# One decoder block on one core: the SBUF pad is left out and the arena of working tiles has 69 tiles, not 68

## The chip, the core and the metric

The kernel runs on one core of a Trainium2 chip. The metric is the time on the device in microseconds (us). The kernel before took 1007.3 us in the median of three runs (1007.09 to 1009.21).

A core has five engines that work beside each other: PE (TensorE, matmuls; its loads of the stationary operand are listed as PEld), DVE (VectorE), ACT (ScalarE), POOL (GpSimd) and SP (SyncE, which issues DMAs here). Each runs its own instructions in a fixed order and waits for others by semaphores. SBUF is the memory that the engines work on; PSUM is the memory that PE writes.

## The reference

One layer of a decoder trunk on 512 tokens of width 1024, batch 1, in float32:

```
h = rmsnorm(x)
h @ w_in  ->  gated linear attention (q, k, v, output gate, forget gate)
              dilated attention, 3 groups of 4 heads (window, dilation) (128,1) (512,4) (2048,16)
              two merge gates
A = gated linear attention in chunks of 64 tokens, 4 heads, dk 128, dv 256
B = the three groups, combined by their softmax denominators
x += (sigmoid(gA) * (A @ w_o_gla) + sigmoid(gB) * (B @ w_o_attn)) @ w_out
x += relu(rmsnorm(x) @ w_mlp1)^2 @ w_mlp2
x += sigmoid(rmsnorm(x) @ w_pg) * (p @ w_pp)
out = rmsnorm(x)
```

For a chunk, with decays a, the gated linear attention carries a state S = diag(a) S + k^T v from chunk to chunk and gives o = q S (the kernel works it out for pairs of chunks).

## The kernel before

Every large product is made of matmuls on numbers that are split into a high part (`hi`, rounded) and a low part (`lo`, the rest): three matmuls hi·hi, hi·lo, lo·hi per tile (`three`, L239 issues them). Weights come in 209 pieces of 128 x 1024 by DMA into the six buffers `w`; for each piece ACT makes `hi` (L225) and DVE makes `lo` (L220). Many of the projections use a scheme of seven products instead of eight (`strassen`), with sums of weight pieces made by DVE (L205, L211) and by DMAs that add to what is in `w` (L197, L208).

The order of each engine's instructions is that of the program. PE runs the large products in pieces of 8 matmuls (`run`), and after each piece `step()` lets the side work go one step: generators in the list `side` (two at a time) and small functions in `later`. So the small matmuls and the DVE and ACT work of the attention parts are interleaved with the large products. Waits on an engine hold up all that stands behind.

The side work of this case is `gla(h)`, one generator for each of the four heads of the gated linear attention. Heads 2 and 3 run together, beside the large products of the merge gate `gb` (410 to 460 us of the profiled run). In a head's program: transposes of the keys (L855), the chunk products (L861, L863), the sums of k^T v of pairs (L876 and L887, recorded at L815), the states after one, two and three pairs `s[1]`, `s[2]`, `s[3]` (L884, L885, L889; DVE), their high parts `ss[p][:, 0:256]` (L891; ACT) and low parts `ss[p][:, 256:512]` (L894; DVE), and the outputs (`outs`, matmuls recorded at L815), which read `ss`. L344 is the low part of an operand of these products (`split_lo`), L329 the addition of a finished product to a sum (`add`), L1006 the sigmoid of a gate.

Memory: pools of SBUF follow each other. `const` and `st` hold small tiles; then the pad (L146); then `wst` (the six `w`), `wsp` (5 `hi`, 4 `lo`, 4096 bytes in each partition), and `ar`, the arena: `NU` tiles of 128 x 512 numbers, 2048 bytes in each partition, named `u` or, for split operands, `ur`. All other working tiles are taken from the arena when the program asks for one and given back after their last use. Who gets a tile that another has had waits until the readers and writers of the former one have passed. In the built program before, the first `w` begins at byte 26624 of the partition, `hi` at 51200, `lo` at 71680 and the arena at 88064, all multiples of 2048; of the small tiles, `rstd` begins at 21248 and 23296, `ones_r` at 19616, `ident` at 17408 and `whs` at 18080. The most arena tiles in use at one time, in program order, are 68 of 68; that is in the stretch of `gla(2)` and `gla(3)`.

Of the kernel before, what the change touches and what calls it, by code (L numbers as in the profile page):

```python
# [10 lines left out]
F32 = mybir.dt.float32  # L11
# [8 lines left out]
P = 128  # L20
# [106 lines left out]
C_LN2, C_LN3, C_BA, C_GN, C_LN1, C_LO, C_N = 0, 8, 16, 20, 28, 36, 38  # L127
W0, W12 = 384, 256

NU, NW, PIECE, WAYS = 68, 5, 8, 2  # L130

NPAD = 208

NRAW = 6

# [4 lines left out]
def block_kernel(ctx, tc, xT, ws, pT, wts, wha, wa2, vec, lnf, rel, onehot, ident_d, mask_d, out):  # L140
# [2 lines left out]

    const = ctx.enter_context(tc.tile_pool(name="const", bufs=1))
    st = ctx.enter_context(tc.tile_pool(name="st", bufs=2))
    const.tile([P, NPAD], F32, name="pad")  # L146
    wst = ctx.enter_context(tc.tile_pool(name="wst", bufs=NRAW))
    wsp = ctx.enter_context(tc.tile_pool(name="wsp", bufs=1))
    ar = ctx.enter_context(tc.tile_pool(name="ar", bufs=NU))
# [1218 lines left out]
```

## Time and profile before

| | before |
|---|---|
| median of three runs | 1007.3 us (1007.09 to 1009.21) |
| the profiled run, its own time | 1008.85 us |
| its span, first to last instruction | 1006.7 us |
| PE busy | 984.2 us (98%) |
| DVE busy | 673.6 us (67%) |
| ACT busy | 525.9 us (52%) |
| mean granted clock of PE | 0.991 |

The page gives the busy time of each engine and then the same in 40 equal slices of some 25.2 us, a digit for tenths, and a row PEclk with the granted clock of PE in tenths (1.0 is 2.4 GHz, 0.5 is 1.2 GHz). A view of windows gives these numbers for any stretch; the timeline gives single instructions, with the idle time of the engine before them and what ended it in brackets. A busy PE isn't a PE at its peak: matmuls overlap, and their ends are modelled.

### The profile page before, as it was taken

Reading aid. Unit: us, or ns where it says so; the run is one execution under the profiler, and the core shown is the slowest. Engines: PE = TensorE matmul, PEld = TensorE weight load, DVE = VectorE, ACT = ScalarE, POOL = GpSimd, SP = SyncE. Lnnn points to the kernel's source line nnn. Section 1 sums busy time; section 2 is a strip of 40 time slices with the busy share of each in tenths; the row PEclk is TensorE's granted clock in tenths of the full one; section 3 lists DMA queues with packets and bytes.
Section 4 is the critical chain, followed back from the end, with each engine's and each line's share of the span. In section 5 each row is a group of like instructions: output and inputs, shape, how many; then the busy total and the mean of one; then the engine's idle time right before and its main releaser. Section 6 shows DMA issues by size and latency. Waiting matters only on the chain.

```text
span 1006.7 us, 15530 instructions
## 1 busy us (share of the span) xinstructions
PE 984.2 (98%) x6228; PEld 898.8 (89%) x6228; DVE 673.6 (67%) x948; ACT 525.9 (52%) x875; POOL 80.4 (8%) x116
## 2 busy tenths in 40 slices
PE   9999999999999999889999999999999999999996
PEld 7788999999998999879988888999998888888885
DVE  7776675566677677858955689778877544743553
ACT  7335547645546665646632346655666434443633
POOL 0230000010000101012002001101000000000000
PEclk9999999999999999979999999999999999999999
DMA  8463461463366355426536425665654322433102
GB/s 303 129 212 83 106 173 40 103 147 106 86 167 167 115 133 146 112 63 177 163 121 193 121 63 148 156 179 131 163 147 147 89 100 81 151 103 102 46 1 84
DMA packets 38168, 127.31 MB, mean 126 GB/s; under 512 B 4883, under 2 KB 6495, under 8 KB 38096
## 3 DMA queue, kind: packets, MB, share of 16 engines
q1 hardware_dynamic: 27504, 92.51, 28.3%
q0 software_dynamic: 8864, 30.66, 15.6%
q10 hardware_dynamic: 1728, 3.15, 0.8%
q8 instruction: 49, 0.80, 0.3%
q14 instruction: 23, 0.19, 0.1%
HBM read 122.06 MB, written 6.07 MB: 127 GB/s over the span
## 4 chain that ended last, share of the span: by engine, by line
PE 91%; DVE 5%; issue 2%; ACT 1%; DMA 0%; POOL 0%; SPq 0%; POOLq 0%; DVEq 0%; ACTq 0%
PE mmt L239 73%; PE smt L239 9%; PE smt L815 2%; DVE lo L220 1%; PE smt L759 1%; PE smt L686 1%; PE smt L861 1%; PE mmt L453 1%; DVE w L205 0%; PE mmt L454 0%; DMA u<-in_xT_dram 0%; PE mmt L452 0%; PE smt L863 0%; PE smt L776 0%; PE smt L775 0%
## 5 line engine op out<-in xcount | busy, mean ns | idle before, releaser
L239 PE MATMUL mmt<-ur,hi 128*128 128x256 f32 (+1 forms) x2784 | 610.3, 315 | 0.0
L239 PEld LDWEIGHTS mmt<-ur,hi 128*128 128x128 f32 x2784 | 461.4, 192 | 31.8 <-issue 1.9
L239 PE MATMUL mmt<-ur,lo 128*128 128x256 f32 (+1 forms) x1392 | 438.0, 315 | 0.5 <-DVE lo L220 0.5
L220 DVE TENSOR_TENSOR lo<-w,hi 128x1024 fp32r<-128x1024 f32 x230 | 278.9, 1221 | 121.8 <-PE mmt L239 71.9
L225 ACT ACTIVATE hi<-w 128x1024 fp32r<-128x1024 f32 x230 | 240.7, 1053 | 133.1 <-issue 65.1
L239 PEld LDWEIGHTS mmt<-ur,lo 128*128 128x128 f32 x1392 | 266.6, 191 | 16.4 <-DVE lo L220 0.9
L239 PE MATMUL mmt<-hi,ur 128*128 128x256 f32 (+1 forms) x640 | 156.1, 334 | 0.0
L336 ACT ACTIVATE ur<-u 128x512 fp32r<-128x512 f32 x136 | 80.2, 621 | 91.6 <-DVE u L1036 30.9
L239 PEld LDWEIGHTS mmt<-hi,ur 128*128 128x128 f32 x640 | 119.8, 215 | 5.6
L344 DVE TENSOR_TENSOR ur<-u,ur 128x512 fp32r<-128x512 f32 x135 | 89.0, 688 | 26.9 <-ACT ur L336 22.7
L239 PE MATMUL mmt<-lo,ur 128*128 128x256 f32 (+1 forms) x320 | 106.1, 332 | 0.6 <-DVE lo L220 0.6
L239 PE MATMUL smt<-ur,hi 128*128 128x512 f32 x272 | 83.7, 389 | 0.0
L311 ACT ACTIVATE u<-mmt 128x512 f32<-128x512 f32 x84 | 49.9, 594 | 53.5 <-PE mmt L239 52.9
L329 DVE TENSOR_TENSOR u<-u,mmt 128x512 f32<-128x512 f32 (+1 forms) x84 | 52.5, 652 | 29.2 <-PE mmt L239 29.1
L239 PEld LDWEIGHTS mmt<-lo,ur 128*128 128x128 f32 x320 | 68.8, 215 | 3.6 <-DVE lo L220 1.0
L239 PEld LDWEIGHTS smt<-ur,hi 128*128 128x128 f32 x272 | 51.1, 188 | 10.6
L239 PE MATMUL smt<-ur,lo 128*128 128x512 f32 x136 | 53.0, 390 | 0.0
L208 POOL DMA_DIRECT2D w<-in_wts_dram x21 | 18.2, 868 | 311.0 <-DVE w L205 234.4
L1146 ACT ACTIVATE u<-u 128x256 f32<-128x256 f32 x64 | 23.0, 409 | 36.5 <-DVE u L1137 36.5
L197 POOL DMA_DIRECT2D w<-in_wts_dram x21 | 18.6, 888 | 204.8 <-DMA w<-in_wts_dram 76.9
L239 PEld LDWEIGHTS smt<-ur,lo 128*128 128x128 f32 x136 | 25.5, 188 | 5.3
L205 DVE TENSOR_TENSOR w<-w 128x1024 f32<-128x1024 f32 x21 | 25.7, 1225 | 0.7
(204 smaller groups left out, 723.4 us busy)
## 6 DMA issues: line engine op xcount, KB each, us to landing
w<-in_wts_dram SPq DMA_DIRECT2D x167, 512.0 KB, 3.8
w<-in_wts_dram POOLq DMA_DIRECT2D x42, 512.0 KB, 5.7
u<-in_xT_dram SPq DMA_DIRECT2D x8, 256.0 KB, 4.6
y_dram<-u ACTq DMA_DIRECT2D x8, 256.0 KB, 2.6
u<-y_dram POOLq DMA_DIRECT2D x8, 256.0 KB, 5.6
u<-in_xT_dram POOLq DMA_DIRECT2D x8, 256.0 KB, 7.4
cb_dram<-c_dram POOLq DMA_DIRECT2D x4, 448.0 KB, 6.2
u<-in_ws_dram SPq DMA_DIRECT2D x8, 192.5 KB, 4.6
```

The lines of the kernel that those rows point to most:

```text
L197: GP.dma_start(w, wts[UNIT[f"{q}.A22"]], accum_op=OP.add)
L205: V.tensor_tensor(w, w, raw[f"{q}.A11"], op=OP.add)
L208: GP.dma_start(w, wts[UNIT[f"{q}.A21"]], accum_op=OP.add)
L220: V.tensor_tensor(lo, w, hi.bitcast(F32), op=OP.subtract)
L225: S.activation(hi, w, AF.Copy)
L239: TE.matmul(o, lhsT=l, rhs=r, start=a, stop=b, skip_group_check=shared)
L311: S.activation(sums[c], bank[b], AF.Copy, scale=-scale if c[0] else scale)
L329: V.tensor_tensor(out, s, ps, op=OP.subtract if m else OP.add)
L336: S.activation(hi, x, AF.Copy)
L344: V.tensor_tensor(lo, x, hi.bitcast(F32), op=OP.subtract)
L815: TE.matmul(o, lhsT=l[a][:, lc], rhs=r[b], start=start and i == 0, stop=stop and i == 2)
L1146: S.activation(hid[j][:, halves(t)], s[:, halves(n)], AF.Square)
```

## The change

The pad of 208 numbers (832 bytes in each partition) is left out, and `NU` is 69. The names of lines above are those of the kernel before; in the kernel after, lines from L134 on stand three lines earlier. In the built program after, the small tiles of `const` and `st` and the large pools begin 832 bytes lower: `w` at 25792, `hi` at 50368, `lo` at 70848, the arena at 87232. Each of these large pools begins 1216 bytes above a multiple of 2048. In the stretch of `gla(2)` and `gla(3)` up to 69 arena tiles are in use.

```diff
@@ -127,9 +127,7 @@
 C_LN2, C_LN3, C_BA, C_GN, C_LN1, C_LO, C_N = 0, 8, 16, 20, 28, 36, 38
 W0, W12 = 384, 256
 
-NU, NW, PIECE, WAYS = 68, 5, 8, 2
-
-NPAD = 208
+NU, NW, PIECE, WAYS = 69, 5, 8, 2
 
 NRAW = 6
 
@@ -143,7 +141,6 @@
 
     const = ctx.enter_context(tc.tile_pool(name="const", bufs=1))
     st = ctx.enter_context(tc.tile_pool(name="st", bufs=2))
-    const.tile([P, NPAD], F32, name="pad")
     wst = ctx.enter_context(tc.tile_pool(name="wst", bufs=NRAW))
     wsp = ctx.enter_context(tc.tile_pool(name="wsp", bufs=1))
     ar = ctx.enter_context(tc.tile_pool(name="ar", bufs=NU))
```

The instructions of every engine are the same and stand in the same order. What differs is which former tile a new one of the arena takes the place of, and so the waits. This is DVE's program in the states of heads 2 and 3, before (the names are out<-in with their numbers; s[2] of head 3 is u_4542, its s[1] u_4541, and ur_4522 is the first `ss` of head 2; in brackets the semaphores waited for, PE_49 being PE's):

```order
L344 TENSOR_TENSOR ur_4518<-u_4340,ur_4484 128x512 [waits DVE_49,PE_49,Activation_49]
L884 COPY u_4520<-smt_4477 128x256 [waits PE_49]
L885 SCALAR_TENSOR_TENSOR u_4521<-u_4520,dab_4259,smt_4477 128x256 [waits DVE_49,Activation_49]
L344 TENSOR_TENSOR ur_4539<-u_4353,ur_4506 128x512
L884 COPY u_4541<-smt_4499 128x256 [waits DVE_49]
L885 SCALAR_TENSOR_TENSOR u_4542<-u_4541,dab_4283,smt_4499 128x256 [waits DVE_49,PE_49]
L220 TENSOR_TENSOR lo_4552<-w_4101,hi_4488 128x1024 [waits DMASW7_49]
L205 TENSOR_TENSOR w_4101<-w_4101,w_4324 128x1024 [waits DVE_49]
L329 TENSOR_TENSOR u_4447<-u_4447,mmt_4271 128x512
L889 SCALAR_TENSOR_TENSOR u_4520<-u_4521,dab_4259,smt_4527 128x256
L889 SCALAR_TENSOR_TENSOR u_4541<-u_4542,dab_4283,smt_4548 128x256
L894 TENSOR_TENSOR ur_4522<-u_4520,ur_4522 128x256 [waits Activation_49]
```

And the same place after (every number of a tile is one lower):

```order
L341 TENSOR_TENSOR ur_4517<-u_4339,ur_4483 128x512 [waits DVE_49,PE_49,Activation_49]
L881 COPY u_4519<-smt_4476 128x256 [waits DVE_49,PE_49]
L882 SCALAR_TENSOR_TENSOR u_4520<-u_4519,dab_4258,smt_4476 128x256 [waits DVE_49,PE_49]
L341 TENSOR_TENSOR ur_4538<-u_4352,ur_4505 128x512 [waits Activation_49]
L881 COPY u_4540<-smt_4498 128x256
L882 SCALAR_TENSOR_TENSOR u_4541<-u_4540,dab_4282,smt_4498 128x256 [waits DVE_49]
L217 TENSOR_TENSOR lo_4551<-w_4100,hi_4487 128x1024 [waits DMASW7_49]
L202 TENSOR_TENSOR w_4100<-w_4100,w_4323 128x1024 [waits DVE_49]
L326 TENSOR_TENSOR u_4446<-u_4446,mmt_4270 128x512
L886 SCALAR_TENSOR_TENSOR u_4519<-u_4520,dab_4258,smt_4526 128x256
L886 SCALAR_TENSOR_TENSOR u_4540<-u_4541,dab_4282,smt_4547 128x256
L891 TENSOR_TENSOR ur_4521<-u_4519,ur_4521 128x256 [waits Activation_49]
```

No row has moved. The second state of head 3 (L885, after: L882) waited for PE and no longer does: before, its tile is one that an operand of head 2's first output matmuls had (`smt_4634`); after, it is one that head 3's own `at` had, which PE doesn't read. The first row waits for PE in both, but by the values of the semaphores for different matmuls: before, for head 3's group of the third pair; after, for head 2's group ahead of it.

## Rows read from the trace of the kernel before

**Rows 1.** The page: PE's busy time, and its granted clock in 40 slices.
```profile
PE 984.2 (98%) x6228; PEld 898.8 (89%) x6228; DVE 673.6 (67%) x948; ACT 525.9 (52%) x875; POOL 80.4 (8%) x116
...
PEclk9999999999999999979999999999999999999999
```

**Rows 2.** Waits of PE, whole run: engine line <- releaser: us, times, longest.
```profile
PE smt L815 <- DVE ur L894: 4.4, 2, 3.7
```

**Rows 3.** Windows: length, busy (count) of PE, PEld, DVE, ACT, POOL, PEclk, DMA, GB/s.
```profile
408.30:411.54 3.24, 0.08 (x2) 0.01 (x1) 3.13 (x8) 3.24 (x8) 1.17 (x3) 1.00 0.00 0
411.54:415.00 3.46, 3.46 (x17) 3.46 (x18) 3.36 (x7) 1.44 (x3) 0.73 (x1) 0.52 0.60 79
435.00:439.82 4.82, 0.64 (x5) 0.23 (x3) 4.56 (x7) 0.42 (x1) 0.85 (x1) 0.91 0.00 0
439.82:449.20 9.38, 8.64 (x38) 8.34 (x39) 7.59 (x12) 7.53 (x22) 0.81 (x1) 0.50 0.54 114
442.00:449.00 7.00, 6.26 (x30) 5.96 (x30) 6.96 (x11) 6.67 (x20) 0.61 (x1) 0.50 0.44 113
611.00:614.00 3.00, 1.47 (x13) 1.26 (x11) 1.09 (x4) 0.67 (x2) 1.89 (x2) 1.00 0.52 153
```

**Rows 4.** Timeline, 427 to 451 us: start, length, instruction [idle before <- releaser].
```profile
427.89 0.52 PE L815 MATMUL smt<-ur 128*128 128x256 f32 x3
...
429.21 0.52 PE L815 MATMUL smt<-ur 128*128 128x256 f32 x3
...
429.71 0.69 DVE L344 TENSOR_TENSOR ur<-u,ur 128x512 fp32r<-128x512 f32 x1 [3.14 <-ACT u L1006]
...
431.96 0.42 DVE L884 COPY u<-smt 128x256 f32<-128x256 f32 x1
...
435.17 0.48 DVE L885 SCALAR_TENSOR_TENSOR u<-u,dab,smt 128x256 f32<-128x256 f32 x1 [2.79 <-PE smt L815]
...
435.29 0.42 ACT L891 ACTIVATE ur<-u 128x256 fp32r<-128x256 f32 x1 [5.28 <-PE smt L815]
...
439.35 0.42 DVE L894 TENSOR_TENSOR ur<-u,ur 128x256 fp32r<-128x256 f32 x1
...
439.82 0.79 PE L815 MATMUL smt<-ur 128*128 128x256 f32 x2 [3.68 <-DVE ur L894]
...
440.65 0.42 ACT L891 ACTIVATE ur<-u 128x256 fp32r<-128x256 f32 x1 [4.95 <-PE smt L815]
...
444.55 0.80 PE L815 MATMUL smt<-ur 128*128 128x256 f32 x2 [0.74 <-DVE ur L894]
...
446.86 2.64 PE L815 MATMUL smt<-ur 128*128 128x256 f32 x12
...
450.29 1.60 PE L815 MATMUL smt<-ur 128*128 128x256 f32 x12
```

**Rows 5.** By line: tiles at multiples of 2048 bytes; count | busy us, mean ns | idle.
```profile
L239 PEld LDWEIGHTS mmt<-ur,lo 128*128 128x128 f32 x1392 | 266.6, 191 | 16.4 <-DVE lo L220 0.9 <-issue 0.4
...
L344 DVE TENSOR_TENSOR ur<-u,ur 128x512 fp32r<-128x512 f32 x135 | 89.0, 688 | 26.9 <-ACT ur L336 22.7 <-ACT u L1006 3.1 <-PE smt L861 0.6
...
L311 ACT ACTIVATE u<-mmt 128x512 f32<-128x512 f32 x84 | 49.9, 594 | 53.5 <-PE mmt L239 52.9 <-PE smt L855 0.4
```

**Rows 6.** By tile, of `rstd` and of `ones_r`: count: ns min/median/max, first and last start.
```profile
L395 PEld LDWEIGHTS smt<-ur,ones_r x2: 186/186/187, 28.6 to 614.0; 128*128 128x128 f32 x2
...
L1137 DVE SCALAR_TENSOR_TENSOR u<-u,rstd x32: 683/688/693, 618.8 to 765.9; 128x512 f32<-128x512 f32 x32
...
L398 ACT ACTIVATE rstd<-smt x2: 597/598/598, 29.5 to 616.7; 128x512 f32<-128x512 f32 x2
```

**Rows 7.** Waits of the first 32 us, as rows 2.
```profile
ACT ur L440 <- DMA u<-in_ws_dram: 1.5, 2, 0.8
```

**Rows 8.** DMA issues: engine, count, KB each, median us to landing.
```profile
whs<-in_wha_dram SPq DMA_DIRECT2D x1, 128.0 KB, 3.6
...
ident<-in_ident_dram SPq DMA_DIRECT2D x1, 64.0 KB, 4.3
```

## The prediction

> **What bounds the kernel now.** I read the page first: PE is busy for 984.2 of 1006.7 us [rows 1]. So the kernel is bound by PE almost throughout, and a change can only pay where PE stands still or is slow. The row of PE's granted clock shows one such place: one 7, in the slice from 428 to 453 us, and a 9 (90% or more) in all others [rows 1]. The waits of PE over the whole run name the same place: the longest item is 4.4 us for L894, DVE's low part of a state of the gated linear attention, in two waits, the longer 3.7 us [rows 2].
>
> Then the windows around it [rows 3]. From 408.30 to 411.54 us PE does 0.08 us of work; directly after it the clock is 0.52 for 3.46 us. From 435.00 to 439.82 us PE does 0.64 us, and from 439.82 to 449.20 us the clock is 0.50, which is the 1.2 GHz level. So each of these two stalls is paid twice: once as idle time, once as work at half clock. In 611 to 614 us PE is idle for 1.53 us of 3, and the clock there is 1.00.
>
> Last the timeline of the second stall [rows 4]. PE stops at 436.1 us and starts again at 439.82 us, when L894 on DVE ends (439.35 + 0.42 us). What held DVE up is ahead of that: L885 of head 3 waited until 435.17 us, 2.79 us, for PE's L815, though the value that it works on was there at 432.38 us (L884, 431.96 + 0.42). That wait is for the memory: the tile that L885 writes is the one that an operand of the output matmuls had, which PE reaches only at 434.4 us. PE waits for DVE, and DVE waits for PE to give back a tile.
>
> **The change part by part.** The instructions and their order stay, on every engine and queue: no DMA is issued earlier or later in program order, nothing is added. Two things change.
>
> First, the arena. In the stretch of heads 2 and 3 the arena is full, 68 of 68, and with one tile more the tiles change hands differently. The edited waits, one after the other:
>
> - L344 (429.71 us, after an idle 3.14 us [rows 4]) took the tile of an operand of head 3's group of L815 that begins at 429.21 us; now it takes one of head 2's group at 427.89 us, which ends at 428.41 us. It can run some 1.2 us earlier, outside the chain that follows. The profile puts that idle time down to L1006; by the built program the later release was PE's.
> - The five DVE instructions from L344 to the second L884 take 429.71 to 432.38 us, 2.67 us. With L344 done before, four are left; L344 is some 0.6 us from start to start, so about 2.06 us. The first of them, L884, still needs operands of the group at 429.21 us to be given back, by about 429.65 us. So the second L884 ends at about 431.7 us.
> - L885 of head 3 has no wait for PE any more and runs at about 431.65 us, not 435.17 us: 3.5 us earlier.
> - Behind it on DVE stand L220, L205, L329, two L889 and L894, back to back: 435.17 to 439.77 us, 4.60 us. The new end of L894 is 431.65 + 4.60 = 436.25 us. Its other input, L891 on ACT (435.29 us, after 5.28 us idle), still waits for the output matmuls, whose first ends around 435.1 us; so it ends at 435.6 us, in time for L894 at 435.8 us.
> - PE, which stops at 436.1 us, then goes on at 436.3 us: of 3.68 us, some 0.2 us are left.
>
> What is late next is the second wait, 0.74 us at 444.55 us, for the L894 of head 3 [rows 4]. The second L891 stood behind a tile of the first one (440.65 us, idle 4.95 us); now its tile is given back at about 435.25 us, so DVE's chain here isn't held up a second time: from 439.77 to 444.50 us it took 4.73 us with 1.33 us and 0.48 us of waits for ACT in it, and without the first of these DVE comes to the end of that L894 about 4.85 us earlier, at 439.65 us. PE, at full clock, is there before, and waits some 0.9 us. So from here PE is 4.85 us ahead of before: that is the first term.
>
> The second term is the clock. Idle stretches of 0.2 and 0.9 us are shorter than the 1.53 us after which the clock stayed at 1.00 [rows 3], so I let it stay. Of the slow work, the part up to 444.55 us is already in the first term (PE waits for DVE there). The rest, 444.55 to 449.20 us, is 4.65 us. The same twelve matmuls of L815 take 2.64 us at the low level (446.86 us) and 1.60 us at the full one (450.29 us) [rows 4], a ratio of 0.61; 4.65 x 0.39 = 1.8 us. The bounds: nothing, if DVE, which is busy for 6.96 of the 7 us from 442 to 449 us [rows 3], can't go faster; and, with half the busy time of the whole slow window, 8.64 / 2 = 4.3 us, beside both stalls, 3.68 + 0.74 us, in all 8.7 us. I take 1.8, since the twelve matmuls are the nearest rows.
>
> The first big stall, 408.30 to 411.54 us, stays: its chain on DVE (3.13 of 3.24 us busy [rows 3]) waits for no arena tile, before or after. Waits change at many other places too, but in the rest of the run PE's idle time isn't behind an arena tile, so these cost and bring nothing on PE.
>
> Second, the addresses. All pools, the small tiles too, begin 832 bytes lower, so the distances among them are the same; what is new is that the large tiles begin 1216 bytes above a multiple of 2048. Is a tile slower that doesn't begin at such a multiple? The kernel before has a few. `rstd` begins 768 bytes above one: DVE reads it in 688 ns (L1137) against 688 ns for L344, ACT writes it in 598 ns against 594 ns for L311. `ones_r` begins 1184 bytes above one, and its load as stationary operand takes 186 ns against 191 ns [rows 5, 6]. So the price is nothing for three of four kinds of access, bounded by 4 of 594 ns, 0.7%, at most; below nothing, by 5 of 191 ns on a load that matmuls cover. No row shows the fourth, PE's moving operand. I take 0 and keep the rest as a rival. For the DMAs, `whs` begins 160 bytes above a multiple of 256 and lands in 3.6 us, `ident` at a multiple, half the size, in 4.3 us [rows 8]: no price to be seen. I take 0 to 0.3 us, since ACT waits 1.5 us for the first loads in all [rows 7] and a few per cent of a landing would go there.
>
> The Trainium skill, "DMA: Bandwidth & Descriptors", section "How a descriptor splits into AXI transactions", speaks against the change: a descriptor that doesn't begin at a multiple of 256 bytes costs more beats. For rows of 4096 bytes that begin 192 bytes above one, my estimate from that page is 134 beats, not 128, for 2048 bytes 70, not 64. By that rule every load would be 5 to 9% longer; the landing of `whs` doesn't show it, and the weights are loaded well ahead of their use, so the sum would change by the 0.3 us above at most.
>
> The sum: 4.85 + 1.8 = 6.65 us less. On the profiled execution (1008.85 us, its span 1006.7 us) that gives 1002.2 and 1000.1 us. The median of the runs is 1.55 us under that execution, so I take it off the median: 1007.3 - 6.65 = 1000.65, and with 0.15 us for the first loads 1000.8 us.
>
> **The rivals.**
>
> A. The stall goes, but the clock falls all the same. For it: some idle time stays, in two pieces close to each other, and the first big stall shows how the clock falls. Against it: 1.53 us of idle time at 611 us without a fall. PE would go on at 436.3 us at half clock, arrive at DVE's data without waiting, and keep 4.4 to 4.85 us: 1002.6 us.
>
> Beside this rival: the Trainium skill, "TensorE: Matmul & The Clock Gate", section "A second HAM failure mode: psum-queue depth-cycling", says that short idle times, when they come often, can make the clock swing. By that rule it would be A; the window at 611 us doesn't agree, but there the idle time comes in one place.
>
> B. The wait is only moved. L891 waits for PE in both kernels, and the state of head 2 has to pass ACT and DVE behind it. If L220 and L205 (2.45 us between them) still came behind that wait, PE would stand as long as before: no change, 1007.3 us. Against it: L894 is DVE's seventh instruction after L344, and no wait for PE is left in front of L220.
>
> C. The new addresses cost PE. Its moving operand is the one access without a row. Twelve matmuls of 256 columns in 1.60 us are 0.52 ns a column; if a start off a multiple of 128 bytes (1216 is 64 above one) cost one more fetch of 32 columns of which half is of no use, 16 columns, that is 8.3 ns, and 6228 matmuls make 52 us: 1053 us. It decides from 6.65 us / 6228 = 1.07 ns per matmul, two columns. At the 0.7% of ACT's row it would be 6.9 us, and the gain is just gone: 1007.7 us. For it: nothing in the rows excludes it. Against it: the three other accesses, PE's stationary one among them.
>
> **How the numbers follow.** A measurement of this kernel tells about 0.2% (2 us) from no change. The forecast gets 0.6, its own range 999.0 to 1002.4 us (the clock's term between 0 and 3.4); A 0.12; B and the near-cancelled form of C together 0.08; C as a loss 0.17; the rest, 0.03, is the full 8.7 us, 998.5 us. Faster: 0.6 + 0.12 + 0.03 = 0.75; same 0.08; slower 0.17. The range takes in the full gain and A and reaches into B: 998.3 to 1006.3 us, with C left out.
>
> **What would show it.** Right: PE's wait for L894 at 436 us falls from 3.7 to some 0.2 us; L885 of head 3 starts right behind L884; the clock reads 1.00 from 415 us on; the stall at 408 us and its slow 3.46 us are still there; PE's busy time falls, since slow work goes. A: the wait gone, a clock of 0.50 after 436 us all the same. Wrong: an equal PE wait at another instruction (B), or matmuls of L239 with a larger mean and longer times in stretches without any wait (C), which one window of the later products would show.

## The result and the profile after

The kernel after takes 1001.17 us in the median of four runs (1000.51 to 1003.71), the kernel before 1007.47 us (1007.09 to 1009.21) beside it: a ratio of 0.9939, with a 95% interval from 0.9918 to 0.996. The forecast was 1000.8 us. The profiled run of the kernel after is the longest of its four: 1003.71 us, span 1001.9 us, mean granted clock 0.993; the others took 1000.51 to 1001.28 us at 0.995 and 0.996. Lines stand three earlier than before: L885 is L882, L891 is L888, L894 is L891, L815 is L812.

From the page, PE's busy time and its clock, as [rows 1]:

```profile
PE 982.5 (98%) x6228; PEld 897.4 (90%) x6228; DVE 673.1 (67%) x948; ACT 524.9 (52%) x875; POOL 80.3 (8%) x116
...
PEclk9999999999999999899999999999999999999999
```

PE has 1.7 us less to do although it runs the same matmuls: some of them ran at half clock before. The slice with a 7 is gone; an 8 stands in the slice ahead of it, from 401 to 426 us, with the first big stall. The longest waits of PE in the run, as [rows 2] (engine line <- releaser: us, times, longest):

```profile
PE smt L852 <- DVE u L840: 2.9, 1, 2.9
PE smt L392 <- ACT ur L333: 1.6, 1, 1.6
PE smt L812 <- DVE ur L891: 1.3, 2, 1.0
```

The wait of 3.7 us isn't among them; the two waits for this line are now 0.26 and 1.02 us. The windows of [rows 3], and one more (length, busy time and count of PE, PEld, DVE, ACT, POOL, then PEclk, DMA, GB/s):

```profile
408.30:411.54 3.24, 0.33 (x3) 0.29 (x3) 3.13 (x8) 3.24 (x8) 1.89 (x3) 0.82 0.00 0
411.54:415.00 3.46, 3.46 (x18) 3.46 (x17) 3.36 (x10) 1.39 (x4) 0.00 (x0) 0.50 0.85 144
...
435.00:439.82 4.82, 3.71 (x27) 3.11 (x25) 4.34 (x9) 3.17 (x9) 0.85 (x1) 1.00 0.53 75
439.82:449.20 9.38, 8.82 (x73) 8.83 (x74) 6.65 (x13) 8.76 (x29) 3.73 (x4) 1.00 0.43 131
...
609.00:612.00 3.00, 3.00 (x16) 2.90 (x16) 2.88 (x3) 3.00 (x5) 0.00 (x0) 0.54 0.95 203
```

From 439.82 to 449.20 us the clock is 1.00 where it was 0.50, and PE gets 73 matmul records done, not 38. The stall at 408 us and its slow work are still there. The last row is new: a stall of PE at 606 us (the second wait above) is followed by half clock, which the like stall before wasn't (1.00 from 611 to 614 us, [rows 3]). The timeline, as [rows 4] (start, length, instruction, idle before it):

```profile
431.96 0.42 DVE L881 COPY u<-smt 128x256 f32<-128x256 f32 x1
432.42 0.48 DVE L882 SCALAR_TENSOR_TENSOR u<-u,dab,smt 128x256 f32<-128x256 f32 x1
...
435.15 0.88 PE L812 MATMUL smt<-ur 128*128 128x256 f32 x6
435.95 0.72 ACT L888 ACTIVATE ur<-u 128x256 fp32r<-128x256 f32 x2 [5.47 <-PE smt L812]
...
436.59 0.75 DVE L891 TENSOR_TENSOR ur<-u,ur 128x256 fp32r<-128x256 f32 x2
...
437.06 0.50 PE L812 MATMUL smt<-ur 128*128 128x256 f32 x2 [0.26 <-DVE ur L891]
...
440.38 0.50 PE L812 MATMUL smt<-ur 128*128 128x256 f32 x2 [1.02 <-DVE ur L891]
...
441.68 1.60 PE L812 MATMUL smt<-ur 128*128 128x256 f32 x12
...
444.07 1.60 PE L812 MATMUL smt<-ur 128*128 128x256 f32 x12
...
607.80 0.50 PE L392 MATMUL smt<-ur,ones_r 128*128 128x512 f32 x1 [1.57 <-ACT ur L333]
608.53 0.80 PE L393 MATMUL smt<-ur,ones_r 128*128 128x512 f32 x1 [0.22 <-DVE ur L341]
```

L882 of head 3 starts 0.46 us behind L881, without a wait; before, it stood 2.79 us. The group of twelve matmuls that took 2.64 us takes 1.60 us.

Where the time went: this execution comes to the group at 435.15 us 0.78 us later than before (434.37 us), since the slow work behind the first stall lasted longer in it. It leaves the first wait 2.76 us earlier (437.06 against 439.82 us), the second 4.17 us (440.38 against 444.55 us) and comes to the last group 6.22 us earlier (444.07 against 450.29 us). Matmul by matmul it then stays 6.2 us ahead up to 606 us, so the other waits that changed bring PE nothing. At 606 us it gives back some 1.4 us to the clock; its span is 4.8 us shorter. The profiled run of e2_pad_69 below, with the same waits and a clock of 1.00 behind 606 us, is level with before when it comes to the first group (0.04 us late), 7.0 us ahead at the last one, and keeps that to the end: a span of 999.8 us against 1006.7.

### The profile page after: what moved, and what is told of

It is laid out like the page before. It is cut to its first block, busy times and chain, and to the rows that moved or that the text cites. A ratio compares the mean times of both kernels' runs of the same rounds, so it can differ in the third digit from the quotient of the medians.

```text
span 1001.9 us, 15523 instructions
## 1 busy us (share of the span) xinstructions
PE 982.5 (98%) x6228; PEld 897.4 (90%) x6228; DVE 673.1 (67%) x948; ACT 524.9 (52%) x875; POOL 80.3 (8%) x116
## 4 chain that ended last, share of the span: by engine, by line
PE 91%; DVE 5%; issue 2%; ACT 1%; DMA 0%; POOL 0%; SPq 0%; POOLq 0%; DVEq 0%; ACTq 0%
PE mmt L236 73%; PE smt L236 9%; DVE lo L217 1%; PE smt L812 1%; PE smt L756 1%; PE smt L683 1%; PE smt L858 1%; PE mmt L450 1%; DVE w L202 0%; PE mmt L451 0%; PE mmt L449 0%; DMA u<-in_xT_dram 0%; PE smt L860 0%; DVE ur L341 0%; PE smt L773 0%
## 5 line engine op out<-in xcount | busy, mean ns | idle before, releaser
L217 DVE TENSOR_TENSOR lo<-w,hi 128x1024 fp32r<-128x1024 f32 x230 | 278.9, 1220 | 123.9 <-PE mmt L236 72.3
L222 ACT ACTIVATE hi<-w 128x1024 fp32r<-128x1024 f32 x230 | 240.4, 1053 | 132.0 <-issue 65.3
L333 ACT ACTIVATE ur<-u 128x512 fp32r<-128x512 f32 x136 | 80.2, 621 | 89.3 <-DVE u L1033 30.9
```

What stands on the lines that cost most here:

```text
L217: V.tensor_tensor(lo, w, hi.bitcast(F32), op=OP.subtract)
L222: S.activation(hi, w, AF.Copy)
L333: S.activation(hi, x, AF.Copy)
```

## The experiments

| kernel | what differs | median us | ratio to before, 95% |
|---|---|---|---|
| e1_nopad_68 | after, 68 tiles | 1008.43 | 0.9999 (0.999 to 1.0008) |
| e2_pad_69 | after, large pools at 0 | 1001.70 | 0.9937 (0.9925 to 0.995) |
| e3_off1248 | after, large pools at 1248 | 1001.86 | 0.9935 (0.9923 to 0.9947) |
| e4_own_tile | before, a tile of its own for one state | 1002.60 | 0.9945 (0.9932 to 0.9959) |
| e5_fill | before, PE kept at work in the stall | 1007.67 | 0.9997 (0.9988 to 1.0005) |
| e7_70tiles | after, 70 tiles | 1002.22 | 0.9937 (0.9925 to 0.9949) |
| e6_yields | after, two products put later | 1002.78 | 0.9947 (0.9935 to 0.9959) |
| e3b_unequal | after, arena at another offset than the weights | 994.98 | 0.9867 (0.9853 to 0.9881) |
| e9_hi64_lo128 | the same, other distances | 1004.30 | 0.9961 (0.9948 to 0.9973) |
| e10_hi256_lo32 | the same, other distances | 1007.40 | 0.9991 (0.9982 to 1.0) |
| e11_gap192 | the same, other distance | 998.50 | 0.9894 (0.9872 to 0.9917) |
| e12_gap320_rms | e3b's distance, one product later | 993.66 | 0.9857 (0.9841 to 0.9874) |

### Is it the tile or the addresses?

```diff
 # e1_nopad_68, against after
-NU, NW, PIECE, WAYS = 69, 5, 8, 2
+NU, NW, PIECE, WAYS = 68, 5, 8, 2
 # e2_pad_69, against before
-NU, NW, PIECE, WAYS = 68, 5, 8, 2
+NU, NW, PIECE, WAYS = 69, 5, 8, 2
-        bc = const.tile([P, T], F32, tag="rstd", name="rstd", bufs=2)
+        bc = const.tile([P, T], F32, tag="rstd", name="rstd", bufs=1)
 # e3_off1248, against after
+NPAD = 8
+    const.tile([P, NPAD], F32, name="pad")
```

> The addresses of the changed kernel (no padding) with the 68 tiles of before: the semaphores that each instruction waits for are those of before. Theory 'the tile': the wait of PE's L815 (L812 here) for DVE's L891 near 436 us is back at 3.7 us with the low clock of 439.8 to 449.2 us behind it, and the time is that of before, 1007.0 to 1007.8. Rival 'the addresses': the gain came with the removed padding, and the time is 1000.5 to 1002, with a wait that is still 3.7 us.

> The padding of before (the large pools begin at 0 within 2048 bytes) with the 69 tiles of the changed kernel; room for both is made by one buffer of rstd in place of two. Theory 'the tile': no 3.7 us wait near 436 us, full clock from 439.8 to 449.2 us, 1000.5 to 1002. Rival 'the addresses': 1006.5 to 1008. If the single rstd buffer costs something, it shows at the next L217 behind an rstd, and is under 0.5 us.

> 69 tiles and a padding of 32 bytes: the large pools begin at 1248 within 2048 bytes (in the changed kernel at 1216), so no longer at a multiple of 64. Theory 'offsets cost nothing': 1000.5 to 1002, and the L236 matmuls keep their means of 283 to 402 ns. Rival 'the engines read a tile in lines of 64 bytes or more': a share of every read is added, of which even 1% of PE's 982 us would be 10 us: 1005 to 1020.

Measured: 1008.43, 1001.70 and 1001.86 us, beside 1008.34 us of before. The two edits fall apart cleanly: the tile alone brings 6.6 us, the addresses alone nothing. (e1 is above its window of 1007.0 to 1007.8 us, and so is before itself beside it.) At offsets of 0, 1216 and 1248 bytes the times with 69 tiles are 1001.7, 1001.2 and 1001.9 us. In e1's trace the wait is back, 3.7 us, with a clock of 0.50 behind it. That execution was granted 0.85 of the clock elsewhere and took 1075.97 us, so the place lies some 25 us later; only these rows are read from it (PE's waits, and a window):

```profile
PE smt L812 <- DVE ur L891: 4.4, 2, 3.7
...
463.00:473.00 10.00, 7.35 (x32) 7.06 (x33) 8.15 (x15) 6.54 (x18) 0.85 (x1) 0.50 0.50 107
```

The rows of the kernel after that answer to [rows 5] are the same to 2 ns:

```profile
L236 PEld LDWEIGHTS mmt<-ur,lo 128*128 128x128 f32 x1392 | 266.8, 192 | 16.3 <-DVE lo L217 0.9 <-issue 0.4
...
L341 DVE TENSOR_TENSOR ur<-u,ur 128x512 fp32r<-128x512 f32 x135 | 89.0, 686 | 25.1 <-ACT ur L333 21.9 <-issue 2.7
L308 ACT ACTIVATE u<-mmt 128x512 f32<-128x512 f32 x84 | 49.9, 594 | 56.5 <-PE mmt L236 56.2
```

### Is it the one wait?

```diff
 # e4_own_tile, against before (and rstd with one buffer)
+    own = const.tile([P, T], F32, name="own")
-        s = [None] + [u32() for _ in range(2)]
+        s = [None, u32(), own if h == 3 else u32()]
```

> The kernel before with 68 tiles and its padding; only head 3's product s[2] (L885 of before) gets a tile of its own, in the room of one rstd buffer, so that this one instruction no longer waits until PE has read the tile's last user. Theory 'it is this one wait': the 3.7 us wait of L815 near 436 us shrinks to under 1.5 us and the clock stays up to 449 us; 1000.5 to 1002.5. Rival 'several relaxed waits make the gain together': the time stays between, 1003 to 1006. Rival 'it was the addresses': 1007 to 1008.

Measured: 1002.60 us, 5.7 us less than before; the window of the forecast is missed by 0.1 us. The timeline around the state and its waits (`own` is the tile):

```profile
429.85 0.69 DVE L344 TENSOR_TENSOR ur<-u,ur 128x512 fp32r<-128x512 f32 x1 [3.14 <-ACT u L1007]
...
432.55 0.48 DVE L886 SCALAR_TENSOR_TENSOR own<-u,dab,smt 128x256 f32<-128x256 f32 x1
...
437.20 0.50 PE L816 MATMUL smt<-ur 128*128 128x256 f32 x2 [1.04 <-DVE ur L895]
...
440.51 0.50 PE L816 MATMUL smt<-ur 128*128 128x256 f32 x2 [1.02 <-DVE ur L895]
```

So 5.7 of the 6.6 us hang on the wait of one instruction, and the clock stays up behind it. The other 0.9 us are within the noise of the two medians; in the traces 0.78 us of them are the first wait, 1.04 us here and 0.26 us in the kernel after. DVE comes to that state later, because the L344 ahead of it still has its old wait (idle 3.14 us, as in [rows 4]).

### Is the clock a term of its own?

```diff
 # e5_fill, against before: matmuls by zeros in front of the sum that waits
+                if p == 1 and h == 2:
+                    for _ in range(NFILL):
+                        TE.matmul(o, lhsT=zr, rhs=qps[0][:, 0:256], start=False, stop=False)
```

> The kernel before with 68 tiles; in the 3.7 us in which PE waits for L894 near 436 us it is given 28 matmuls 128x128 by 128x256 of zeros, added into the sum that follows, so that it waits no shorter but isn't idle (the result is unchanged). Padding is cut by the 512 bytes of the zero tile. Theory 'the wait and then the clock behind it': the wait's own length stays, the clock from 439.8 to 449.2 us stays at 1.00, and 1.8 us of the 6.6 come back: 1005.5 to 1007 against 1008.3 of before. Rival 'the slower clock there is hidden or costs nothing': 1007.5 to 1009. Rival 'the fill delays the sum behind it': above 1009.

Measured: 1007.67 us against 1008.08, not to be told apart. The stretch shows the term all the same (L913 is the fill):

```profile
435.22 0.88 PE L817 MATMUL smt<-ur 128*128 128x256 f32 x6
435.94 3.52 PE L913 MATMUL smt<-ur,zr 128*128 128x256 f32 x28
...
440.67 0.50 PE L817 MATMUL smt<-ur 128*128 128x256 f32 x2 [1.10 <-DVE ur L896]
...
448.82 1.60 PE L817 MATMUL smt<-ur 128*128 128x256 f32 x12
```

and the window of the work behind the stall, with its clock of 1.00 (before: 0.50):

```profile
439.82:449.20 9.38, 6.63 (x51) 6.23 (x52) 7.82 (x15) 7.38 (x22) 0.70 (x2) 1.00 0.50 112
```

From the first group to the end of the stall it is 5.45 us in both kernels (440.67 - 435.22; 439.82 - 434.37), so the wait wasn't shortened. From there to the last group it is 8.15 us at full clock against 10.47 us: 2.3 us for the clock, where the forecast had 1.8. In the medians most of this is missing (0.4 us). In the profiled pair the kernel is 0.41 us late at 18 us (e2's execution, without a zero tile, is 0.35 us late there, e4's isn't), and at 435 us it is 0.85 us late, since its slow work behind the first stall lay differently; so its span is 1.2 us shorter. The expectation that 1.8 us would show in the time failed.

A second measure needs no edit: the 17 runs of before beside this kernel don't have one clock. Eight with a mean clock of 0.991 took 1008.5 us on average, four with 0.994 took 1007.1: 1.4 us between executions of one program.

### Would a 70th tile bring more, and other work in the stalls that are left?

```diff
 # e7_70tiles, against after (and rstd with one buffer)
-NU, NW, PIECE, WAYS = 69, 5, 8, 2
+NU, NW, PIECE, WAYS = 70, 5, 8, 2
 # e6_yields, against after
-        for _ in range(2 + gap):
+        for _ in range(2 + 2 * gap):
+        for _ in range(2 if h > 1 else 0):
+            yield
         vh = ...
```

> The changed kernel with one more arena tile, 70 (one rstd buffer makes room). Theory 'PE's waits that are left are for DVE's own chain or for values just made, not for a tile': 1001 to 1002, the waits at 408 and 436 us as with 69. Rival 'each further tile takes a wait away': under 1000.

> The changed kernel with two more turns of other work between the decay of heads 2 and 3 and their transposes (L852), and between the sum of squares and the broadcast of the rms scale (L392), so that PE has other instructions in the two waits that are left at 408 us (2.9 us with 3 us at half clock behind it) and 606 us (1.6 us). Theory 'what is left is of the same kind, a wait and then the clock': the wait at 408 us under 1 us, the one at 606 us under 1 us; 996 to 998.5. Rival 'the turns only move the wait, since the same engines are late later': 1000 to 1003. Rival 'the turns break the order that the tiles and queues are tuned for': above 1004.

Measured for e7: 1002.22 us, no gain over 69 tiles in the median. Its profiled run (999.95 us) shows one all the same:

```profile
433.89 1.00 PE L812 MATMUL smt<-ur 128*128 128x256 f32 x7
435.27 0.50 PE L812 MATMUL smt<-ur 128*128 128x256 f32 x2 [0.39 <-DVE ur L891]
...
438.02 0.51 PE L812 MATMUL smt<-ur 128*128 128x256 f32 x2 [0.46 <-DVE ur L891]
...
441.72 1.60 PE L812 MATMUL smt<-ur 128*128 128x256 f32 x12
```

From the first group to the last it is 7.83 us, against 8.92 us with 69 tiles (444.07 - 435.15), so the waits at 436 us aren't those of 69 tiles, as the first theory had it. The six runs spread from 999.95 us at a clock of 0.995 to 1003.36 us at 0.991, more than this 1.1 us; whether it reaches the total isn't shown.

Measured for e6: 1002.78 us, no gain over the kernel after (0.9947 against 0.9939). Two of its waits of PE:

```profile
PE mmt L236 <- DVE lo L217: 4.2, 5, 2.5
PE smt L812 <- DVE ur L893: 3.2, 1, 3.2
```

and in its timeline the place of the first:

```profile
414.22 0.39 PE L236 MATMUL mmt<-ur,lo 128*128 128x256 f32 x1 [2.53 <-DVE lo L217]
```

The rival was right for the transposes: at 408 us PE does other work first and then waits 2.5 us for the next low part of a weight, which DVE makes late, since DVE is the chain there; and with heads 2 and 3 put back the wait at 442 us is 3.2 us again. The other edit worked: no wait for L333 at 606 us is left.

### Do the offsets matter against each other?

```diff
 # e3b_unequal: 832 bytes, after with rstd of one buffer; e11_gap192: 192 bytes, two buffers; e12_gap320_rms: 320 bytes, two buffers
     wsp = ctx.enter_context(tc.tile_pool(name="wsp", bufs=1))
+    gap = ctx.enter_context(tc.tile_pool(name="gap", bufs=1))
+    gap.tile([P, NPAD], F32, name="pad")
     ar = ctx.enter_context(tc.tile_pool(name="ar", bufs=NU))
 # e9, e10: lo in a pool of its own, a gap ahead of it (64, 288 bytes) and one behind it (384, 480 bytes)
 # e12, besides: the edit at 606 us of e6
-        for _ in range(2 + gap):
+        for _ in range(2 + 2 * gap):
```

> 69 tiles; the padding stands between the weight pools and the arena, so that the weight tiles begin at 1216 and the arena tiles at 0 within 2048 bytes: the large pools no longer at equal offsets. One rstd buffer makes room. Theory 'offsets cost nothing, equal or not': 1001 to 1002, as e2_pad_69 (1001.7), L225 and L220 (which read a weight tile and write another) at their 1.04 and 1.22 us. Rival 'reads and writes at unequal offsets are slower': DVE's L220 and ACT's L225 longer, or L239's means above 283 to 402 ns, and 1003 or more.

Measured: 994.98 us, 6.7 us less than e2_pad_69 with the same waits. Neither theory had this. DVE's L221 and ACT's L226 keep their means (1221 and 1054 ns against 1220 and 1053 ns); PE's matmuls don't. By line, e2_pad_69 and then e3b_unequal (count | busy us, mean ns):

```profile
L239 PE MATMUL mmt<-ur,hi 128*128 128x256 f32 x2016 | 370.2, 285 | 0.0
...
L239 PE MATMUL mmt<-ur,hi 128*128 128x512 f32 x768 | 238.9, 391 | 0.0
```

```profile
L240 PE MATMUL mmt<-ur,hi 128*128 128x256 f32 x2016 | 360.4, 280 | 0.0
...
L240 PE MATMUL mmt<-ur,hi 128*128 128x512 f32 x768 | 240.7, 394 | 0.0
```

256 columns are faster and 512 slower. It is seen better in the starts. At 650 us, in a stretch without waits, e2_pad_69 and then e3b_unequal:

```profile
650.00 0.40 PE L239 MATMUL mmt<-ur,hi 128*128 128x256 f32 x2
650.24 0.28 PE L239 MATMUL mmt<-ur,lo 128*128 128x256 f32 x1
650.36 0.40 PE L239 MATMUL mmt<-ur,hi 128*128 128x256 f32 x2
...
651.08 0.28 PE L239 MATMUL mmt<-ur,hi 128*128 128x256 f32 x1
```

```profile
650.18 0.40 PE L240 MATMUL mmt<-ur,hi 128*128 128x256 f32 x2
650.42 0.28 PE L240 MATMUL mmt<-ur,lo 128*128 128x256 f32 x1
650.53 0.40 PE L240 MATMUL mmt<-ur,hi 128*128 128x256 f32 x2
...
651.24 0.28 PE L240 MATMUL mmt<-ur,hi 128*128 128x256 f32 x1
```

Nine matmuls in 1.08 us, against nine in 1.06 us. I took the time from each start of a matmul of L239 to the next from the traces (pairs under 300 ns apart, means; the few pairs of 256 columns at half clock are in them and raise the means of w by 0.2 to 0.8 ns). They are sorted by the distance in memory, within 512 bytes, from the operand that is streamed to the one that is loaded for the next matmul; the operands and addresses are those of the built programs. Four more kernels followed from it.

> As e3b_unequal (69 tiles, one rstd buffer), but other distances: hi begins 64 and lo 128 bytes behind the arena tiles, counted within 512 bytes (e3b: both 192; all kernels with equal offsets: 0). In e3b_unequal PE's matmul of 256 columns starts 118 ns after the one before it where the weights to be loaded lie 192 behind the columns that are streamed, and 115 ns where they lie 320 behind; with equal offsets 121.6; 512 columns go the other way, 229 and 234 against 227.4. Theory 'the distance within 512 bytes sets it': 64 and 128 give values of their own, on the hi and the lo matmuls apart, and the time lies between 990 and 1001. Rival 'any unequal distance does the same': 118 and 229 again, 994 to 996. Rival 'it is where the arena begins in itself (0 in e3b)': back to 121.6 and 227.4, 1001 to 1002.

> As e9, with hi 256 and lo 32 bytes behind the arena tiles within 512 bytes. Theory 'the distance within 512 bytes sets it': values of their own for 256 and 32. If the distance counts within 256 bytes, hi (two matmuls of three) is back at 121.6 and 227.4 ns, and the time at 999 to 1002; if within 512, it is not, and 990 to 997. Rival 'any unequal distance does the same': 994 to 996.

> The changed kernel with 192 bytes between the weight tiles and the arena, so that both hi and lo begin 320 bytes behind the arena tiles within 512; two rstd buffers, all waits as in the changed kernel. So far, 320 was seen only where weights are streamed and an arena tile is loaded: 115.3 ns between matmuls of 256 columns and 234 for 512. Theory 'the distance within 512 bytes from what is streamed to what is loaded sets it, whichever of the two is the weight': now the main body (2979 matmuls of 256 columns, 1522 of 512) is at 115.3 and 234, the reversed ones at 118 and 229; 121.4 to 115.3 is -18 us, 227 to 234 is +10, so 990 to 994. Rival 'it matters which of the two is the weight': the main body is at other values, 119 to 122, and 997 to 1004.

> The changed kernel with two edits. First 320 bytes between the weight tiles and the arena, so that hi and lo begin 192 bytes behind the arena tiles within 512 as in e3b_unequal, but the arena at 1536 within 2048 (there 0) and two rstd buffers. Second, the two more turns of e6_yields at the rms scale alone, which put L392 18 matmuls later. Theory 'the distance, not the place of the arena, made e3b_unequal fast': the main body at 118 and 229 ns between matmuls of 256 and 512 columns, worth 6 to 7 us; and 'the turns at 606 us help by themselves': no wait of L392 (1.6 us), worth 1 to 1.7 us: together 992.5 to 995.5. Rival 'it was the arena at 0': intervals of 119 to 122 and 998 to 1001. Rival 'executions of one kernel with unequal offsets fall into two groups, as in e11_gap192 (995.7 and 1001.3)': some runs near 993, some near 999.

Measured, in ns from start to start; "w" is a weight tile loaded while an arena tile is streamed, "a" the reverse. e2: distance 0; e9: hi 64 and lo 128 (a: 448 and 384); e10: hi 256 and lo 32 (a: 256 and 480); e3b and e12: 192 (a: 320); e11: 320 (a: 192). The last row has the plain loads alone; loads that take every fourth number, which some of the arena tiles have, are left out of it.

| distance | 0 | 32 | 64 | 128 | 192 | 256 | 320 | 384 | 448 | 480 |
|---|---|---|---|---|---|---|---|---|---|---|
| w, 256 columns (2979 pairs in all) | 121.4 | 119.1 | 119.6 | 121.2 | 118.2, 117.8 | 120.9 | 117.8 | | | |
| w, 512 columns (1522) | 227.1 | 238.4 | 232.5 | 228.5 | 229.0, 229.0 | 230.6 | 233.3 | | | |
| a, 256 columns (547) | 120.3 | | | | 116.4 | 117.3 | 115.3, 116.4 | 115.6 | 119.4 | 120.5 |
| a, 512 columns (198) | 227.7 | | | | 229.4 | 228.9 | 233.1, 233.1 | 232.1 | 231.5 | 235.8 |

Arena tile against arena tile, always at distance 0, stays at 120.6 to 121.6 ns and 227.5 to 228.4 ns in all these kernels; that is the control, though a small one (some 115 and 70 pairs, nearly all of other lines; the 14 that stand next to a matmul of L239 do move, from 120.0 ns in e2 to 114.1 in e3b). The sum for e3b: 2979 x 3.2 ns and 547 x 5.0 ns are 12.2 us less, the 512s 4.3 us more, 7.9 us in all; PE's busy time fell by 7.6 us (980.8 to 973.2). For e9 the same sum gives 2.3 us more, and PE's busy time rose by 2.3 us. For e10 it gives 5.8 us more; its median is 5.7 us above that of e2, but PE's busy time rose by 7.3 us (988.1) in the profiled run, the longest of its eleven.

So "any unequal distance" falls (e9 and e10 are slower than e2), "where the arena begins" falls (e2 has it at 0 within 2048 as e3b does, without its values, and e12 at 1536, with them), and a period of 256 falls: between two matmuls by hi at full clock, where both distances are 256, e10 has 118.5 and 232.3 ns for 256 and 512 columns, e2 119.9 and 227.1. Within 512 bytes e3b and e12 have both operands at the same two places, so with the same roles only the distance 0 was measured at more than one pair of places (e2, after and e3). The times forecast for e9, e10 and e11 by this theory were all missed; that of e12 held. The one trace of e11 speaks against "whichever of the two is the weight": 320 gives 117.8 ns there for w, and 115.3 for a in e3b.

The distance to the next operand isn't all of it. In e9 and e10 two distances alternate, and the operand loaded before counts as well: e9's 232.5 ns at 64 is the mean of 235.6 where the matmul itself is by hi and 229.3 where it is by lo. And one program has two speeds: e11's six runs lie in two groups, 995.65 to 995.99 us and 1001.0 to 1001.54 us, at the same clock of 0.995 to 0.996; the profile is from the second. Its sum, some 2.7 us less than e2, goes with PE's busy time there (978.6 us, 2.2 us less). What differs between the groups wasn't found, and of the first there is no trace, so its pace by distance isn't known.

e12 is faster than both kernels: 993.66 us, 14.6 us under before. Of its 7.5 us against after some 6 are the distance and the rest the wait at 606 us, as e3b (994.98 us) stands between. Its longest waits of PE and the window around 606 us:

```profile
PE smt L854 <- DVE u L842: 3.2, 1, 3.2
...
PE smt L814 <- DVE ur L893: 1.6, 2, 1.0
```

```profile
602.00:612.00 10.00, 10.00 (x87) 10.00 (x86) 9.83 (x13) 6.70 (x12) 0.86 (x1) 1.00 0.66 171
```

## Why the prediction was right, and where not

- The stall of 3.68 us was to shrink to 0.2 us: it is 0.26 us. L885 of head 3 was to start right behind L884: it does. e4 shows that this instruction's wait was the cause, with 5.7 of 6.6 us.
- The first term was 4.85 us: 4.17 us at the second wait, and with the 0.78 us by which this execution came late, 4.95 us. The second wait was put at 0.9 us and is 1.02 us.
- L344, released early, was counted with 0.6 us in that chain: 0.78 us by the waits of e4 (1.04 - 0.26), 0.9 us by its time.
- The second term, the clock, was 1.8 us: from 4.17 to 6.22 us ahead, 2.05 us; 2.3 us in e5.
- The reason given for it doesn't hold: "Idle stretches of 0.2 and 0.9 us are shorter than the 1.53 us after which the clock stayed at 1.00". In the profiled run of the kernel after PE stood idle for 1.57 and 0.22 us at 606 us, and the clock was 0.54 from 609 to 612 us; in e2's run, with 1.55 and 0.23 us there, it was 1.00 in the same window. One execution's row was no bound. The step itself held: behind the waits left at 436 and 440 us the clock was 1.00 in the traces of after, e2, e3, e4 and e7. That much of it was luck, since the row it went by didn't secure it.
- The addresses were 0: right for pools that stay at equal offsets (e1, e2, e3). For PE's streamed operand that 0 had no row behind it. The 0.15 us for the first loads didn't come: ACT waits 1.3 us for them after, 1.5 before.
- The rule named from the Trainium skill, "DMA: Bandwidth & Descriptors", section "How a descriptor splits into AXI transactions", shows no price here: the 167 loads of weights that SP issues begin at a multiple of 256 bytes before and 192 above one after, and land in 3.8 us before and 3.7 after (medians). `whs`, which the prediction went by, begins off such a multiple in both kernels and says nothing on it.
- Rival C: its reason fell, since the start of a tile in itself costs PE nothing. But "the one access without a row" was the right place to doubt. PE's pace does hang on addresses, on distances between operands; the change left them at zero, and e9 and e10 show 2.6 and 5.7 us of loss when they move, against the 6.3 us of the whole change. A (the clock falls at 436 us) and B (the wait moves) didn't happen; a move as in B came in e6.
- Two slips on which nothing hangs: L894 is DVE's eighth instruction behind the second L344, not the seventh; and 1000.8 us with the clock's term between 0 and 3.4 us is 999.2 to 1002.6 us, not 999.0 to 1002.4.

## What to carry to other kernels

In a kernel whose busiest engine stands at 98%, look for the wait in which two engines wait for each other through a tile that is only given back late: one more tile was worth 6.6 us here, and a tile of its own for one value 5.7 us. A stall was paid here in idle time and then, often, in work at half clock; the second part came and went from execution to execution, so one row without it is no proof that it stays away. Measure the distance between the operand that is streamed and the one that is loaded before settling a layout: equal offsets weren't the best here.

## What the hardware showed that was not expected

- The pace of these matmuls hangs on where the loaded operand lies against the streamed one: 115.3 to 121.4 ns for 256 columns and 227.1 to 238.4 ns for 512. At most distances that help the one, the other loses. Why is open.
- An arena tile of which every fourth number is loaded makes a matmul of 512 columns slower: 235.0 to 235.2 against 227.7 ns in e2, 237.9 to 238.0 against 233.1 ns in e3b. Whether the first number lies 0, 4, 8 or 12 bytes into the tile makes no difference (39 to 44 pairs each).
- One program with unequal distances, e11, ran at two speeds at the same granted clock: 995.8 and 1001.4 us in the mean, three runs each.
